# Four of the seven sums of an FFN block's products are formed in PSUM, and ScalarE copies them out

## The chip, the core and the metric

The kernel runs as one program on one core of a Trainium2 chip. The metric is the device time of that program in microseconds (us); less is better. The engines are named as in the profile: PE is TensorE, DVE is VectorE, ACT is ScalarE, POOL is GpSimd, SP issues the DMAs. SBUF is the working memory, PSUM the accumulators that PE writes.

## The reference, cut to what matters

The reference is one layer of a network: three token mixers (SSD, mLSTM, GLA), a gated merge, an output projection, then a SwiGLU FFN on 512 latent tokens with 1024 channels, and a last norm. Only the first half of the FFN is touched:

```
h = rmsnorm(x) modulated            # 512 tokens x 1024 channels
g, u = split(h @ W_in)              # 2816 columns each
a = silu(g) * u                     # then a @ W_out, the residual, the last norm
```

The kernel takes the 2816 columns as 22 blocks of 128 (blocks f = 0 to 21): a block has 128 columns of the gate g and 128 of the other factor u, over all 512 tokens.

## The kernel before, in words

Every number that PE multiplies is split into a high part (a cast by ACT to the type that PE multiplies fast) and a low part (what the cast left out, a subtraction on DVE or POOL). A product of two split operands takes three matmuls: high by high, high by low, low by high.

Blocks 0 and 1 are plain products (`halves()`). Blocks 2 to 21 (`for f in range(FC, KF)`, lines L1852 and after) save multiplications. With the block's weights as four quadrants A11, A12, A21, A22 (g or u columns by lower or upper channels), POOL forms the sums S1 = A21 + A22, S2 = S1 - A11, S3 = A11 - A21 and S4 = A12 - S2 (`weight_sums`, line L1635, 128x512 each; `FE1 = "GGGG"` puts all four on POOL). Of the eight matrices, seven are multiplied with a matching sum of tokens: A11, S1, S2, A12, S3, A22, S4. A product is 12 matmuls of 128x256 (`product`, L1849), so PE issues 84 matmuls in an iteration. The four results of a block (g and u, each for the lower and the upper 256 tokens, `lo` and `hi`) are sums of these seven products:

```
m  = A11;  r = m + S2;  v = r + S3
g[lo] = m + A12          g[hi] = r + S1 + S4
u[lo] = v + A22          u[hi] = v + S1
```

Ahead of each product `prepare()` issues one weight sum of the next block and `part(p)` for the product four places on (`FD = 4`): ACT casts the high part (L1806 in the kernel before, L1810 in the one after), and DVE or POOL subtracts for the low part (L1807, then L1811) as the letter of `FE2` says (V is DVE, G is POOL; the letter stands for the place in `order`). After the last product of an iteration `gate()` forms tanh(g/2) on ACT (L1769) and two products on DVE (L1770 and L1772, 128x512). For f below `FE0 = 4` it also splits its result at once (a cast on ACT, L362, and a subtraction, L363).

Weights, their sums and their parts live in 23 tiles of 128x512 called `w0` to `w22`, taken and given back in a ring: a cast, a sum or a subtraction that writes such a tile waits for the last reader of what stood there. In PSUM there are three tiles called `acc` and five called `bank`.

PE runs in the order of the program text. The other engines' instructions are put in an order by a scheduler before the program is built. That order is fixed, and each engine takes its own instructions in it, one by one, so whatever stands behind a waiting instruction waits too.

Of the kernel before, what the change touches and what calls it, by code (L numbers as in the profile page):

```python
# [9 lines left out]
F32 = mybir.dt.float32  # L10
# [4 lines left out]
OP = mybir.AluOpType  # L15
# [25 lines left out]
KV = 6  # L41
# [16 lines left out]
FE2 = "VVGVVGV"  # L58
# [34 lines left out]
class Slots:  # L93
    """A unit's share of the working tiles of phase one; what it puts back it can take again."""
# [18 lines left out]
    def pieces(self, c):  # L113
        """A tile of class c, cut into tiles of 512 columns."""
        t = self.get(c)
        return [t[:, j:j + 512] for j in range(0, SIZE[c] - 511, 512)]
# [11 lines left out]
    def close(self, *keep):  # L128
        """Everything is given back but for the tiles kept."""
        names = {t.tensor.name for t in keep}  # L130
        for n in [n for n in self.out if n not in names]:
            c, i = self.out.pop(n)
            self.net.free[c].append(i)
        for c, z in self.own.items():
            self.net.free[c].extend(z)
            z.clear()


class Net:
# [18 lines left out]
    def crow(self, name, n):  # L158
        """A row of constants on every partition."""
# [39 lines left out]
    def block(self, key):  # L199
        """The weight block of a key, split; fetched before if it was announced."""  # L200
# [7 lines left out]
    def fetch(self, key, now=True, pieces=None):  # L208
        """Starts to load a weight block, or some pieces of it; gives the functions that split them."""
# [35 lines left out]
    def jobs(self, queue, gens=None, then=()):  # L245
        """Runs jobs (weight block, function, ...) in order, the next block on its way, and
        carries the scans on between them."""
# [36 lines left out]
    def ready(self):  # L284
        """The next job: of those that can run, the first whose weights are here."""
# [7 lines left out]
    def push(self, jobs):  # L293
        """Jobs to be run next, behind those of the block that is on its way."""
# [17 lines left out]
    def dense(self, *parts, ks=None):  # L312
        """parts: (PSUM, weights, first column, last, tokens (high, low), first, last)."""
# [23 lines left out]
    def load_x(self):  # L337
        """The residual stream, where the context was."""
# [8 lines left out]
    def tok(self, W, i):  # L347
        """Tokens of tile i (context 0, 1, latents 2..5) on partitions, 256 columns."""
# [23 lines left out]
    def rstd_gen(self, sq, n, scale, cb, rb):  # L372
        """1 / rms of n tokens, on every partition (in rb), from tiles of squares."""
# [25 lines left out]
    def silu_c(self, c):  # L399
        """c (1 + tanh(c / 2)) of the two modulation vectors, on every partition; rows of 128, an  # L400
        identity behind them."""
# [18 lines left out]
    def modulate(self, k, s, silu):  # L420
        """Shift and scale of channels 128 k .. of one vector, by VectorE."""
# [14 lines left out]
    def modulate_pe(self, sc, ws):  # L436
        """Shift and scale of the channels from 128 KV of both vectors, by TensorE."""
# [20 lines left out]
    def scale_in(self, x, n, s, k, H, L, rb, eng):  # L458
        """The modulated norm of channels 128 k .., split."""
# [13 lines left out]
    def conv(self, acc, p, n, w, cc):  # L473
        """SAME convolution of 5 taps over the free axis, scaled by 1/2."""
# [16 lines left out]
    def gates(self):  # L491
        """Columns: decays of the SSD heads, forward and backward (32), of the mLSTM heads (8); the
        latter's input gates behind them. Tokens on partitions, tiles 0, 1 context, 2..5 latents."""
# [154 lines left out]
    def turn_rows(self, own, R, E, n, name):  # L648
        """Two sets of columns as rows over the latents, in DRAM."""
# [379 lines left out]
    def head_turn(self, own, ht, w, columns):  # L1029
        """Channels of a head on partitions, times the norm's gain; from column to row order."""  # L1030
# [257 lines left out]
    def prepare(self, b, Y, H, L, own):  # L1288
        """Splits the output of branch b, channels as they come."""
# [100 lines left out]
    def rstd2(self, c):  # L1390
        """1 / rms of 256 tokens from c on, from the sums of squares."""
# [4 lines left out]
    def late(self):  # L1396
        """The rest of the modulation of the latents."""
# [18 lines left out]
    def startup(self):  # L1416
        """The modulated inputs, and block after block of their channels the first products."""
# [144 lines left out]
    def add_square(self, m, x, c0, c1):  # L1562
        """Adds block m of the channels to the sum of squares, the last one kept apart."""
# [8 lines left out]
    def scale2(self, c, sv, h):  # L1572
        """The modulated norm before the FFN of 256 tokens from c on, in h and split."""
# [15 lines left out]
    def token_sums(self, h):  # L1589
        """With B11, B12 / B21, B22 the quadrants (channels, tokens) of h: T1 = B12 - B11,  # L1590
        T2 = B22 - T1, T3 = B22 - B12 and T4 = B21 - T2, split; per pair of channel blocks
        the tiles (T1, T3) and (T4, T2)."""
# [17 lines left out]
    def weight_sums(self, f, out):  # L1610
        """The quadrants (columns, channels) A11, A12 / A21, A22 of an FFN block and
        S1 = A21 + A22, S2 = S1 - A11, S3 = A11 - A21, S4 = A12 - S2, in steps."""
# [27 lines left out]
    def aup(self, up):  # L1640
        """The decays' weights of a head, three times: their low parts once and the high ones twice."""
# [5 lines left out]
    def small(self, p, c0, c1):  # L1647
        """The rows of the decays, three times: their high parts twice and the low ones."""
# [307 lines left out]
def lay_out(i):  # L1956
# [5 lines left out]
    A = {}  # L1962
# [67 lines left out]
```

## Time and profile before

| what | us |
|---|---|
| three runs | 1529.51, 1531.4, 1534.36 |
| median of them | 1531.4 |
| span of the profiled execution, first to last instruction | 1529.1 |
| FFN-in for blocks 2 to 21 in it, first to last copy at L1858 | 1165.06 to 1387.95 |
| one iteration in its steady part (L1858 at 1270.46, then at 1282.15) | 11.69 |
| DVE, PE, POOL, ACT busy in 1200 to 1250 of it | 49.83, 44.10, 42.35, 20.72 |

The profile gives one execution, by its span; the time of an execution that the runs report is of the same size (the span is 0.4 below the fastest run and 2.3 below the median), so differences worked out inside the span are added to the median. The granted TensorE clock was 0.973 on the mean of the span and 1.00 in the stretch from 1200 to 1250.

### The profile page before, as it was taken

The numbers are of one execution on the slowest core, as the hardware profiler recorded it, in microseconds if no ns is written. First come the engines' busy times: TensorE is split into PE (matmuls) and PEld (weight loads), VectorE is DVE, ScalarE is ACT, GpSimd is POOL, SyncE is SP. The second block draws the span as 40 slices with busy tenths as digits, with TensorE's granted clock in tenths as the row PEclk, the third lists the DMA queues.
The fourth block names the chain that finished last, engine by engine and source line by source line (L and its number), as shares of the span: only waits on it lengthen the run. The fifth ranks groups of instructions, "written<-read, shape, count | busy, mean of one in ns | idle before, by whom it ended". The sixth has DMA issues, their size and how long they took to land.

```text
span 1529.1 us, 22249 instructions
## 1 busy us (share of the span) xinstructions
PE 1406.8 (92%) x8044; PEld 1204.6 (79%) x8044; DVE 1033.0 (68%) x1783; ACT 644.0 (42%) x1191; POOL 587.2 (38%) x465
## 2 busy tenths in 40 slices
PE   5898999999999999998997789899998888888997
PEld 3687889887788886887796767677798888887887
DVE  7958463869684658786666765435369999999332
ACT  4464464553244443334454443333355343436231
POOL 4423432324222123221226353134457888881011
PEclk9998999999999999999999999999989999999999
DMA  6532323233443234354455566666322233223331
GB/s 258 189 105 84 106 69 97 72 97 97 137 126 103 78 96 129 88 129 127 159 173 171 175 210 211 197 201 215 117 77 83 83 94 100 84 84 113 90 90 66
DMA packets 99022, 190.39 MB, mean 125 GB/s; under 512 B 10752, under 2 KB 19472, under 8 KB 97760
## 3 DMA queue, kind: packets, MB, share of 16 engines
q1 hardware_dynamic: 98912, 188.97, 39.8%
q8 instruction: 63, 1.03, 0.3%
q14 instruction: 47, 0.39, 0.1%
HBM read 167.27 MB, written 21.14 MB: 123 GB/s over the span
## 4 chain that ended last, share of the span: by engine, by line
PE 53%; DVE 19%; DMA 8%; issue 6%; ACT 5%; POOL 4%; SPq 0%; DVEq 0%; ACTq 0%; POOLq 0%
PE acc L318 28%; PE acc L1884 7%; PE acc L357 7%; DVE w L1807 6%; DMA w<-in_w_main_dram 4%; PE bank L318 2%; DVE ft L1770 2%; DMA w<-in_w_b_dram 1%; ACT w L1806 1%; ACT w L215 1%; DVE w L217 1%; DMA t<-in_wmodT_dram 1%; PE bank L974 1%; POOL row L1160 1%; DMA gd<-xk 1%
## 5 line engine op out<-in xcount | busy, mean ns | idle before, releaser
L217 POOL TENSOR_TENSOR w<-w,w 128x512 fp32r<-128x512 f32 x125 | 176.2, 1409 | 572.8 <-ACT w L215 499.4
L318 PE MATMUL acc<-hlh,w 128*128 128x512 f32 (+1 forms) x1160 | 390.7, 406 | 5.5 <-ACT hlh L465 1.9
L215 ACT CAST w<-w 128x512 fp32r<-128x512 f32 (+1 forms) x302 | 183.2, 613 | 382.9 <-DMA w<-in_w_main_dram 182.6
L217 DVE TENSOR_TENSOR w<-w,w 128x512 fp32r<-128x512 f32 x177 | 138.6, 785 | 202.7 <-ACT w L215 168.6
L318 PEld LDWEIGHTS acc<-hlh,w 128*128 128x128 f32 x1160 | 225.3, 194 | 59.9 <-ACT hlh L465 2.2
L318 PE MATMUL acc<-hll,w 128*128 128x512 f32 (+1 forms) x576 | 230.7, 400 | 3.7 <-DVE hll L471 1.5
L1635 POOL TENSOR_TENSOR w<-w,w 128x512 f32<-128x512 f32 x80 | 135.7, 1717 | 2.7 <-DMA w<-in_w_ffs_dram 1.9
L318 PEld LDWEIGHTS acc<-hll,w 128*128 128x128 f32 x576 | 111.8, 194 | 28.7 <-DVE hll L471 1.9
L1807 DVE TENSOR_TENSOR w<-w,w 128x512 fp32r<-128x512 f32 x100 | 124.0, 1241 | 0.0
L318 PE MATMUL acc<-t,w 128*128 128x512 f32 x440 | 111.2, 401 | 7.4 <-DVE t L363 2.7
L318 PEld LDWEIGHTS acc<-t,w 128*128 128x128 f32 x440 | 83.2, 190 | 28.9 <-DVE t L363 4.3
L1806 ACT CAST w<-w 128x512 fp32r<-128x512 f32 x140 | 79.1, 618 | 60.9 <-DVE w L1807 50.2
L357 PE MATMUL acc<-w,hlh 128*128 128x256 f32 x512 | 96.6, 289 | 0.0
L1849 PE MATMUL bank<-th,w 128*128 128x256 f32 x480 | 93.4, 283 | 0.1
L1849 PE MATMUL acc<-hlh,w 128*128 128x256 f32 x280 | 59.6, 290 | 29.9 <-DVE w L1807 29.9
L357 PEld LDWEIGHTS acc<-w,hlh 128*128 128x128 f32 x512 | 81.6, 194 | 3.0 <-ACT t L920 1.6
L480 DVE SCALAR_TENSOR_TENSOR cacc<-acc,c_scanc,cacc 128x510 f32<-128x510 f32 (+3 forms) x124 | 77.7, 631 | 6.7 <-ACT cacc L476 5.8
L1849 PEld LDWEIGHTS bank<-th,w 128*128 128x128 f32 x480 | 77.3, 190 | 0.5 <-DVE w L1807 0.3
L1807 POOL TENSOR_TENSOR w<-w,w 128x512 fp32r<-128x512 f32 x40 | 61.5, 1538 | 38.1 <-ACT w L1806 36.2
L357 PE MATMUL acc<-w,hll 128*128 128x256 f32 x256 | 73.4, 287 | 0.0
L1849 PEld LDWEIGHTS acc<-hlh,w 128*128 128x128 f32 x280 | 46.0, 190 | 33.7 <-DVE w L1807 33.7
L1849 PE MATMUL bank<-tl,w 128*128 128x256 f32 x240 | 67.8, 282 | 0.0
(453 smaller groups left out, 3089.5 us busy)
## 6 DMA issues: line engine op xcount, KB each, us to landing
w<-in_w_main_dram SPq DMA_DIRECT2D x180, 256.0 KB, 3.4
w<-in_w_ffs_dram SPq DMA_DIRECT2D x80, 256.0 KB, 3.1
t<-in_wmodT_dram SPq DMA_DIRECT2D x32, 512.0 KB, 4.0
w<-in_w_b_dram SPq DMA_DIRECT2D x48, 256.0 KB, 3.5
xk<-gd SPq DMA_DIRECT2D x40, 256.0 KB, 3.5
w<-in_w_ffo_dram SPq DMA_DIRECT2D x40, 256.0 KB, 2.6
row<-rows SPq DMA_DIRECT2D x16, 512.0 KB, 5.5
wmod<-in_wmod_dram SPq DMA_DIRECT2D x6, 1024.0 KB, 8.3
```

Source lines behind the costliest of these rows:

```text
L215: self.S.copy(h, w)
L217: self.LE[self.wcount % len(self.LE)].tensor_sub(l, w, h.bitcast(F32))
L318: self.T.matmul(dst, w[:, m0:m1], x[:, c0:c1], start=(k == 0 and j == 0), stop=(k == nk - 1 and j == 2))
L357: self.T.matmul(p, x[:, t0:t0 + 128], w, start=(k == 0 and j == 0), stop=(k == KT - 1 and j == 2))
L480: V.scalar_tensor_tensor(acc[:, o0:o1], p[:, o0 + d:o1 + d], w[:, cc, j:j + 1], acc[:, o0:o1], op0=OP.mult, op1=OP.add)
L974: T.matmul(bs[:, :257], kw[d], v[:, 2 + i], start=True, stop=True)
L1635: getattr(next(eng), op)(new(z), x, y)
L1770: V.scalar_tensor_tensor(t, t, 1.0, g, op0=OP.add, op1=OP.mult)
L1806: S.copy(H, x)
L1807: le[p % 7].tensor_sub(L, x, H.bitcast(F32))
L1849: T.matmul(dst, x, y, start=(k == 0 and j == 0), stop=(k == 3 and j == 2))
L1884: T.matmul(po, w, x[:, c0:c1], start=(f == 0 and j == 0), stop=(f == KF - 1 and j == 2))
```

## The change

- The seven products come in another order: A11, S1, S2, A12, S3, S4, A22 instead of A11, S2, S1, A12, S3, A22, S4.
- Three tiles of PSUM are used in an iteration instead of seven. In X the products A11, S2, S3 and A22 are added up one after the other by PE (the first matmul of a later product doesn't clear the tile), so that X holds m, then r, then v, then u[lo]. In Y, S1 and then S4 are added up. Z holds A12.
- ACT copies X out three times (m, r, v) and Y once (`p5`, the product S1) between the products; before, it copied m alone. PE may not add the next product to X or Y until the copy has read it.
- DVE keeps two additions that read PSUM (g[lo] = m + Z, g[hi] = r + Y) where it had seven, and gets one whose operands both lie in SBUF (v + p5, 128x256, which is u[hi]).
- The second instruction of the gate is cut into two of 256 columns: the first reads u[lo] in X (in PSUM), the second reads u[hi] in SBUF. Before, it was one of 512 columns with both operands in SBUF.
- `FE2` is `"VVVGVVG"` instead of `"VVGVVGV"`: read against the two orders, POOL subtracted for S1 and A22 before, and does for A12 and A22 now; DVE does for the other five.
- The tile `fu` is gone, and comments are.

```diff
-FE2 = "VVGVVGV"
+FE2 = "VVVGVVG"
...
-                def gate(f, g, u):
+                def gate(f, g, *u):
...
-                    V.scalar_tensor_tensor(act[f], t, 0.5, u, op0=OP.mult, op1=OP.mult)
+                    c = 0
+                    for z in u:
+                        cs = slice(c, c + z.shape[-1])
+                        V.scalar_tensor_tensor(act[f][:, cs], t[:, cs], 0.5, z, op0=OP.mult, op1=OP.mult)
+                        c = cs.stop
...
-                order = ("A11", "S2", "S1", "A12", "S3", "A22", "S4")
+                order = ("A11", "S1", "S2", "A12", "S3", "S4", "A22")
...
-                def product(f, n, dst):
-                    dst = dst[:, :256]
+                def product(f, n, dst, first=True):
...
-                            T.matmul(dst, x, y, start=(k == 0 and j == 0), stop=(k == 3 and j == 2))
+                            T.matmul(dst, x, y, start=(first and k == 0 and j == 0), stop=(k == 3 and j == 2),
+                                     skip_group_check=True)
...
-                    S.copy(m, product(f, "A11", self.acc_bank()))
-                    V.tensor_add(r, m, product(f, "S2", self.bank()))
-                    p5 = product(f, "S1", self.bank())
-                    V.tensor_add(g[:, lo], m, product(f, "A12", self.acc_bank()))
-                    V.tensor_add(g[:, hi], r, p5)
-                    V.tensor_add(v, r, product(f, "S3", self.bank()))
-                    V.tensor_add(u[:, hi], v, p5)
-                    V.tensor_add(u[:, lo], v, product(f, "A22", self.acc_bank()))
-                    V.tensor_add(g[:, hi], g[:, hi], product(f, "S4", self.bank()))
-                    gate(f, g, u)
+                    X, Y, Z = (z[:, :256] for z in (self.acc_bank(), self.bank(), self.bank()))
+                    product(f, "A11", X)
+                    S.copy(m, X)
+                    product(f, "S1", Y)
+                    S.copy(p5, Y)
+                    product(f, "S2", X, False)
+                    S.copy(r, X)
+                    product(f, "A12", Z)
+                    V.tensor_add(g[:, lo], m, Z)
+                    product(f, "S3", X, False)
+                    S.copy(v, X)
+                    product(f, "S4", Y, False)
+                    V.tensor_add(g[:, hi], r, Y)
+                    V.tensor_add(v, v, p5)
+                    product(f, "A22", X, False)
+                    gate(f, g, X, v)
```

ACT's order in one iteration of the kernel before, block 11, from the tanh of block 10 on (each row: line, operation, tile written, tiles read, size; a number behind a name tells one use of a tile from another):

```order
L1769 ACTIVATE ft_11686<-fg_11538 128x512
L1858 COPY fm_11693<-acc_11696 128x256
L1806 CAST w3_11768<-w7_11655 128x512
L1806 CAST w4_11789<-w12_11747 128x512
L1806 CAST w7_11834<-w19_11661 128x512
L1806 CAST w0_11816<-w5_11727 128x512
L1806 CAST w10_11862<-w13_11766 128x512
L1806 CAST w15_11882<-w22_11659 128x512
L1806 CAST w18_11902<-w6_11787 128x512
```

ACT's order in the same iteration of the changed kernel:

```order
L1769 ACTIVATE ft_11649<-fg_11506 128x512
L1810 CAST w5_11713<-w14_11474 128x512
L1864 COPY fm_11656<-acc_11660 128x256
L1810 CAST w3_11732<-w18_11619 128x512
L1866 COPY fp_11659<-bank_11661 128x256
L1810 CAST w8_11751<-w0_11692 128x512
L1810 CAST w18_11794<-w15_11625 128x512
L1868 COPY fr_11657<-acc_11660 128x256
L1810 CAST w2_11776<-w12_11711 128x512
L1872 COPY fv_11658<-acc_11660 128x256
L1810 CAST w20_11824<-w13_11730 128x512
L1810 CAST w10_11843<-w4_11749 128x512
```

Three copies were put between the casts; the cast of A22 now stands directly behind the tanh, and the copy of r behind the fourth cast, which writes the tile `w18` (before, the third cast, which writes `w7`, had only casts behind it).

DVE's order in the same iteration of the kernel before, from the second product of the gate on:

```order
L1772 SCALAR_TENSOR_TENSOR a10_11689<-ft_11686,fu_11539 128x512
L1807 TENSOR_TENSOR w17_11769<-w7_11655,w3_11768 128x512
L1859 TENSOR_TENSOR fr_11694<-fm_11693,bank_11714 128x256
L1807 TENSOR_TENSOR w8_11790<-w12_11747,w4_11789 128x512
L1862 TENSOR_TENSOR fg_11691<-fr_11694,bank_11734 128x256
L1861 TENSOR_TENSOR fg_11691<-fm_11693,acc_11753 128x256
L1807 TENSOR_TENSOR w21_11835<-w19_11661,w7_11834 128x512
L1863 TENSOR_TENSOR fv_11695<-fr_11694,bank_11774 128x256
L1807 TENSOR_TENSOR w12_11863<-w13_11766,w10_11862 128x512
L1864 TENSOR_TENSOR fu_11692<-fv_11695,bank_11734 128x256
L1865 TENSOR_TENSOR fu_11692<-fv_11695,acc_11795 128x256
L1866 TENSOR_TENSOR fg_11691<-fg_11691,bank_11821 128x256
```

DVE's order in the same iteration of the changed kernel, from the first product of the gate on:

```order
L1770 SCALAR_TENSOR_TENSOR ft_11649<-ft_11649,fg_11506 128x512
L1775 SCALAR_TENSOR_TENSOR a10_11652<-ft_11649,acc_11511 128x256
L1775 SCALAR_TENSOR_TENSOR a10_11652<-ft_11649,fv_11509 128x256
L1811 TENSOR_TENSOR w17_11733<-w18_11619,w3_11732 128x512
L1811 TENSOR_TENSOR w6_11752<-w0_11692,w8_11751 128x512
L1870 TENSOR_TENSOR fg_11655<-fm_11656,bank_11662 128x256
L1811 TENSOR_TENSOR w11_11777<-w12_11711,w2_11776 128x512
L1875 TENSOR_TENSOR fv_11658<-fv_11658,fp_11659 128x256
L1811 TENSOR_TENSOR w0_11825<-w13_11730,w20_11824 128x512
L1874 TENSOR_TENSOR fg_11655<-fr_11657,bank_11661 128x256
L1811 TENSOR_TENSOR w12_11844<-w4_11749,w10_11843 128x512
```

Seven short additions with a PSUM operand (`bank`, `acc`) became two, and one addition between two SBUF tiles (`fv`, `fp`) stands between the third and the fourth subtraction; the first subtraction behind the gate reads `w18`, the tile that ACT's fourth cast writes next.

POOL's order in the same iteration of the changed kernel: two sums (S1, S2), the subtraction for A22, two sums (S3, S4), the subtraction for the next block's A12.

```order
L1635 TENSOR_TENSOR w0_11692<-w11_11621,w22_11623 128x512
L1635 TENSOR_TENSOR w12_11711<-w0_11692,w18_11619 128x512
L1811 TENSOR_TENSOR w1_11714<-w14_11474,w5_11713 128x512
L1635 TENSOR_TENSOR w13_11730<-w18_11619,w11_11621 128x512
L1635 TENSOR_TENSOR w4_11749<-w15_11625,w12_11711 128x512
L1811 TENSOR_TENSOR w7_11795<-w15_11625,w18_11794 128x512
```

Before, POOL's row was subtraction, sum, subtraction, three sums. The subtraction for A12 writes the tile `w7`, which PE reads in product S3 of the same iteration (as `w7_11675`).

## Rows read from the trace of the kernel before

**Rows 1.** The page's first line.

```profile
span 1529.1 us, 22249 instructions
```

**Rows 2.** Busy time by windows: us, PE, PEld, DVE, ACT, POOL, PE clock, DMA.

```profile
1200.00:1250.00 50.00, 44.10 (x366) 43.28 (x366) 49.83 (x59) 20.72 (x40) 42.35 (x26) 1.00 0.31 95
```

**Rows 3.** Groups by shape, 1140 to 1390: busy us, mean ns, idle before.

```profile
L1635 POOL TENSOR_TENSOR w<-w,w 128x512 f32<-128x512 f32 x77 | 131.2, 1725 | 2.0 <-DMA w<-in_w_ffs_dram 1.9
L1807 DVE TENSOR_TENSOR w<-w,w 128x512 fp32r<-128x512 f32 x100 | 124.0, 1241 | 0.0
```

**Rows 4.** Waits, 1160 to 1370: total us, times, longest.

```profile
PE acc L1849 <- DVE w L1807: 24.3, 17, 1.7
```

**Rows 5.** Timeline of DVE: start, length, line, operation.

```profile
1262.23 1.75 DVE L1807 TENSOR_TENSOR w<-w,w 128x512 fp32r<-128x512 f32 x1
...
1264.24 0.68 DVE L1807 TENSOR_TENSOR w<-w,w 128x512 fp32r<-128x512 f32 x1
1264.84 0.41 DVE L1862 TENSOR_TENSOR fg<-fr,bank 128x256 f32<-128x256 f32 x1
1265.17 0.41 DVE L1861 TENSOR_TENSOR fg<-fm,acc 128x256 f32<-128x256 f32 x1
1265.51 1.69 DVE L1807 TENSOR_TENSOR w<-w,w 128x512 fp32r<-128x512 f32 x1
...
1267.45 1.44 DVE L1807 TENSOR_TENSOR w<-w,w 128x512 fp32r<-128x512 f32 x1
...
1269.81 0.78 DVE L1807 TENSOR_TENSOR w<-w,w 128x512 fp32r<-128x512 f32 x1
1270.59 1.71 DVE L1770 SCALAR_TENSOR_TENSOR ft<-ft,fg 128x512 f32<-128x512 f32 x1
1272.33 1.66 DVE L1772 SCALAR_TENSOR_TENSOR a<-ft,fu 128x512 f32<-128x512 f32 x1
1273.91 1.75 DVE L1807 TENSOR_TENSOR w<-w,w 128x512 fp32r<-128x512 f32 x1
```

**Rows 6.** Timeline of POOL, with the idle time before in brackets.

```profile
1265.35 1.30 POOL L1807 TENSOR_TENSOR w<-w,w 128x512 fp32r<-128x512 f32 x1 [1.91 <-ACT w L1806]
1266.61 1.73 POOL L1635 TENSOR_TENSOR w<-w,w 128x512 f32<-128x512 f32 x1
1268.30 1.74 POOL L1807 TENSOR_TENSOR w<-w,w 128x512 fp32r<-128x512 f32 x1
1270.01 5.11 POOL L1635 TENSOR_TENSOR w<-w,w 128x512 f32<-128x512 f32 x3
1277.03 1.29 POOL L1807 TENSOR_TENSOR w<-w,w 128x512 fp32r<-128x512 f32 x1 [1.91 <-ACT w L1806]
```

**Rows 7.** Timeline of ACT in the steady part.

```profile
1264.06 2.70 ACT L1806 CAST w<-w 128x512 fp32r<-128x512 f32 x5 [3.35 <-DVE w L1807]
...
1270.46 0.35 ACT L1858 COPY fm<-acc 128x256 f32<-128x256 f32 x1
...
1282.15 0.36 ACT L1858 COPY fm<-acc 128x256 f32<-128x256 f32 x1
```

**Rows 8.** Timeline of ACT at the stage's start.

```profile
1177.53 0.35 ACT L1858 COPY fm<-acc 128x256 f32<-128x256 f32 x1
...
1181.10 0.62 ACT L362 CAST ah<-ft 128x512 fp32r<-128x512 f32 x1 [2.70 <-DVE ft L1772]
```

**Rows 9.** Timeline of DVE and POOL at 131 and at 839.

```profile
131.50 0.40 DVE L544 TENSOR_TENSOR t<-t,t 128x240 f32<-128x240 f32 x1
131.78 1.70 POOL L217 TENSOR_TENSOR w<-w,w 128x512 fp32r<-128x512 f32 x1 [3.75 <-ACT w L215]
131.82 0.40 DVE L545 TENSOR_TENSOR t<-t,t 128x240 f32<-128x240 f32 x1
...
838.65 0.68 DVE L217 TENSOR_TENSOR w<-w,w 128x512 fp32r<-128x512 f32 x1
...
839.15 1.32 POOL L217 TENSOR_TENSOR w<-w,w 128x512 fp32r<-128x512 f32 x1 [2.56 <-issue]
839.25 2.85 DVE L1085 TENSOR_TENSOR_SCAN t<-mask,t 128x774 f32<-128x774 bf16 x1
```

More of the change, by code (lines that the diff above doesn't have):

```diff
@@ L1848, in product @@
                         for j, (x, y) in enumerate(((w, h), (w, l), (v, h))):
-                            T.matmul(dst, x, y, start=(k == 0 and j == 0), stop=(k == 3 and j == 2))
+                            T.matmul(dst, x, y, start=(first and k == 0 and j == 0), stop=(k == 3 and j == 2),
+                                     skip_group_check=True)
                     self.wput(*slots)
                     next(prep, None)
-                    return dst
                 for f in range(FC, KF):
                     lo, hi = slice(0, 256), slice(256, 512)
-                    g, u = (sp.tile([128, 512], F32, name=n, bufs=2) for n in ("fg", "fu"))
-                    m, r, v = (sp.tile([128, 256], F32, name=n, bufs=2) for n in ("fm", "fr", "fv"))
-                    S.copy(m, product(f, "A11", self.acc_bank()))
-                    V.tensor_add(r, m, product(f, "S2", self.bank()))
-                    p5 = product(f, "S1", self.bank())
-                    V.tensor_add(g[:, lo], m, product(f, "A12", self.acc_bank()))
-                    V.tensor_add(g[:, hi], r, p5)
-                    V.tensor_add(v, r, product(f, "S3", self.bank()))
-                    V.tensor_add(u[:, hi], v, p5)
-                    V.tensor_add(u[:, lo], v, product(f, "A22", self.acc_bank()))
-                    V.tensor_add(g[:, hi], g[:, hi], product(f, "S4", self.bank()))
-                    gate(f, g, u)
+                    g = sp.tile([128, 512], F32, name="fg", bufs=2)
+                    m, r, v, p5 = (sp.tile([128, 256], F32, name=n, bufs=2) for n in ("fm", "fr", "fv", "fp"))
+                    X, Y, Z = (z[:, :256] for z in (self.acc_bank(), self.bank(), self.bank()))
[14 more added lines that the diff above has]
+                    gate(f, g, X, v)
                 for f in range(FE0, KF):
@@ L1920, in final @@
         for h in range(4):
-            o = self.sp.tile([128, 2, 256], F32, name=("ft", "fu")[h % 2], bufs=2)
+            o = self.sp.tile([128, 2, 256], F32, name=("ft", "fg")[h % 2], bufs=2)
             for j in range(2):
```

## The prediction

> **What bounds the kernel now.** I read the page first for the span [rows 1]; the change touches only FFN-in, some 220 us of it. Then the windows: in that stage DVE is busy 49.83 of 50 us, PE 44.10 and POOL 42.35, at a full clock [rows 2]. Read alone, this says that DVE is the bound and that additions taken off it are time won. The groups speak against that: DVE's subtraction of 128x512 takes 1241 ns on the mean [rows 3], while one of the same shape takes 0.68 where it ran alone (at 1264.24) [rows 5]. So I went to the two timelines. From POOL's subtraction at 1265.35 on, DVE and POOL take turns: POOL's 1.30 ends at 1266.65, DVE's subtraction that began at 1265.51 ends at 1267.20, 0.55 later; POOL's next (from 1266.61) ends at 1268.34, 1.14 later; DVE's (from 1267.45) ends at 1268.89, 0.55 later, and so on [rows 5, 6]. An operation of DVE with both operands in SBUF and one of POOL never progress together; each turn is about 1.15 for POOL and 0.55 for DVE. Much of DVE's "busy" is waiting for its turn. The additions that read PSUM don't take part: 0.41, and 0.33 start to start (the one at 1264.84 is followed by another at 1265.17) [rows 5].
>
> One iteration is thus a chain of turns. From POOL's start at 1265.35 to the end of DVE's subtraction at 1273.91 + 1.75 = 1275.66 it has POOL's first 1.30, five more turns of POOL and six of DVE: 1.30 + 5 x 1.15 + 6 x 0.55 = 10.35, and the rows give 10.31. Then it leaves the pair: ACT's cast waited 3.35 for just this subtraction, which frees its tile (seen an iteration earlier: DVE ends at 1262.23 + 1.75 = 1263.98, ACT starts at 1264.06), and two casts later POOL can start its next subtraction at 1277.03, having idled 1.91 [rows 5 to 7]. This detour is 1277.03 - 1275.66 = 1.37. Together 11.68; the copies of m are 1282.15 - 1270.46 = 11.69 apart [rows 7]. PE is no bound, it waits for DVE's subtractions, 24.3 us in 17 waits [rows 4]; a product is 12 x 44.10 / 366 = 1.45, seven are 10.1.
>
> **The change part by part.**
>
> *Five additions with a PSUM operand leave DVE, 5 x 0.33 = 1.65 per iteration, 33 us in 20.* They ran beside POOL's turns: between 1264.84 and 1270 POOL works on while DVE does them [rows 5, 6]. I take them at nothing. If that cover were absent the gain would be the 33.
>
> *The addition v + p5, both in SBUF,* joins the turns with 256 columns. No row has it; its bounds are nothing (the engine waits anyhow) and a full turn, 0.55. I take half, 0.28. *The gate's second product:* of 0.55 in the turns, the half that reads PSUM leaves and the other stays, 0.28. So DVE's turns are 6 x 0.55 + 2 x 0.28 = 3.86 against 7 x 0.55 = 3.85 before, POOL's stay 6 x 1.15 = 6.9. The sum, 10.75, is what the pair needs in either kernel, 0.94 below the 11.69. What the change can win is in the gaps, 0.94 x 17 = 16 us at most.
>
> *The order of the turns.* By the order of the changed kernel, from POOL's subtraction for A12: 1.30, v + p5 0.28, sum S1 1.15, subtraction 0.55, sum S2 1.15, subtraction 0.55. Here the gate's first product stands right behind that subtraction on DVE, and if it goes on at once it takes 0.60 (the pitch from 1264.24 to 1264.84); then POOL's A22 subtraction 1.15, the SBUF half of the gate 0.28, sum S3 1.15, DVE's subtraction that reads `w18` 0.55. Sum 1.30 + 0.28 + 1.15 + 0.55 + 1.15 + 0.55 + 0.60 + 1.15 + 0.28 + 1.15 + 0.55 = 8.71. The last turns (sum S4 and a subtraction) fall into the detour.
>
> *The detour grows.* That subtraction frees the tile for ACT's fourth cast, as its counterpart did before. But now the copy of r stands behind this cast, PE may not add product S3 to X before it, and POOL's subtraction for A12 writes the tile that product S3 reads last. The chain: 0.08 to ACT, cast 0.54 (2.70 / 5), copy 0.35 [rows 7], a hand-over to PE, product 1.45, a hand-over to POOL. The hand-overs I take at 0.13 each, what is left of the old detour after 0.08 and two casts (1.37 - 0.08 - 1.16). Sum 0.08 + 0.54 + 0.35 + 0.13 + 1.45 + 0.13 = 2.68. An iteration is then 8.71 + 2.68 = 11.39, 0.30 less than 11.69. Over the 17 steady intervals: -5.1 us.
>
> The Trainium skill, "Perfetto Trace Analysis", section Matmuls, says that independent matmul groups should rotate through different PSUM banks, so that a copy out of one overlaps the matmuls of the next. The old code does so and the new one chains four products in X. Counted by the rule with nothing overlapped, three copies of 0.35 and two hand-overs of 0.13 each, 0.61 x 3 x 20, would cost 37 us; the order of products here puts another product (1.45) between two of X, which covers 0.61, unless ACT is late.
>
> *The start.* While f < 4 the gate ends in a split whose cast (L362) waits for the gate on DVE, 2.70 [rows 8]. Before, the copy of m stood ahead of it (1177.53 against 1181.10). Two such gates lie in the loop, of blocks 2 and 3. In the changed order the next block's copy of m stands behind this cast, and PE's S2 waits for it. I take 2.5 each, +5; bounds 0 (PE had lost that time anyhow) and 2.7 each, plus one wait of 3.35 in the first iteration, where fewer turns are queued, 8.8.
>
> *The rest:* PSUM has tiles to spare with three in use instead of seven, no DMA is added, the matmuls are the same 84. The three added copies cost ACT 0.35 each [rows 7], at 20.72 of 50 busy [rows 2]: nothing, but for the detour counted above.
>
> The sum: -5.1 + 5 = about 0, on the span of 1529.1 and so on the median of 1531.4. **Forecast: no change, 1531.4 us.** Own range of this case 1526 to 1536: the steady gain could be 0.1 more or less per interval (1.7), the start -5 to +3.8.
>
> **The rivals.**
>
> *POOL takes the pair first (slower).* The place: DVE's subtraction that ends the turn before the gate's first product. The addition g[hi] stands ahead of this subtraction, and ACT's tanh and the A22 cast follow it, 0.41, the tanh at the pitch of a cast of its size, 0.54, the cast 0.62 [rows 8] and two hand-overs that I estimate at 0.05 each, 1.67 from its start; the subtraction, waiting for POOL, starts 0.33 after it and lasts 1.44, 1.77. So POOL's A22 subtraction asks for the pair some 0.1 before DVE is through, and the gate's product asks as DVE goes on. If POOL goes first, its 1.15 comes ahead of the gate, and the chain to the subtraction that frees `w18` becomes 1.30 + 0.28 + 1.15 + 0.55 + 1.15 + 0.55 + 1.15 + 0.55 + 1.15 + 0.28 + 1.15 + 0.55 = 9.81; with 2.68, 12.49, +0.80 per iteration. 17 x 0.80 + 5 = +18.6: 1550. What decides is who wins when POOL asks about 0.1 early. In the one near case POOL began 0.12 before DVE's operation ended (131.78 against 131.90), DVE's next went on at 0.40 and POOL took 1.70, so DVE won; where POOL began 0.18 before the end (839.15 against 839.33), it took 1.32 and DVE's next 2.85, so POOL won [rows 9]. 0.1 lies on DVE's side, by little. Chance 0.28.
>
> A rule beside it: the Trainium skill, "SBUF — State Buffer", section Who interferes with whom, has the shared port pair as an exclusive lock, taken by DVE operations with two SBUF inputs, and lets issue order decide who blocks; the turns of rows 5 and 6 agree (1.15 and 0.55). Taken by the word, POOL's request, issued earlier, would win; the row at 131.78 does not agree with that reading, the one at 839.15 does.
>
> *DVE is the bound after all (faster).* If the chain closes up without the longer detour, the 16 us of gaps are won: 1531.4 - 16 = 1515, or 1520 with the start's +5. For it: DVE's 49.83 of 50, and the 1.65 that leave. Against it: the turns, and that ACT's cast still waits for one subtraction. Chance 0.10.
>
> *PE waits for ScalarE in each chain (slower).* In an iteration the copies of m and v have one product of cover as well; were one of them late as the copy of r is, by another 2.68 - 1.37 = 1.31, that is 1.31 x 17 = 22 us, 1553. For it: ACT is served in order and waits 3.35 at a time [rows 7]. Against it: only one cast per iteration waits so long. Chance 0.05.
>
> *Nothing but noise around the forecast:* 0.57.
>
> **How the numbers follow.** A measurement of this kernel tells changes from 0.3%, 4.6 us, on. The forecast's case (0.57) lies within it but for its edges, 0.06 to the faster side and 0.03 to the slower. So faster 0.10 + 0.06 = 0.16, same 0.48, slower 0.28 + 0.05 + 0.03 = 0.36. The range leaves out the faster rival (0.10) and the upper tail of the slower ones: 1525 to 1551.
>
> **What would show it.** Right: in 1200 to 1350 copies of m 11.3 to 11.5 apart; DVE's additions with PSUM gone and its busy time lower by no more than the stretched operations take; ACT's fourth cast waiting some 2 us with the copy of r behind it and PE waiting about 1.5 for that copy; first two intervals longer than before. Rival one: intervals of 12.5, POOL's A22 subtraction at 1.3 and the gate's first product at 1.7 or more. Rival two: intervals below 11. Wrong altogether: stretched additions that read PSUM, or a clock below 1.00 in the stage.

## The result and the profile after

The changed kernel takes 1554.46 us on the median of four runs (1551.62 to 1558.02), the kernel before 1532.88 in the same comparison: the ratio is 1.0167, with a 95% interval of 1.014 to 1.0194. It is slower by about 22 us. I had forecast no change, 1531.4, and a range to 1551; the time lies on the far side of the range, at the price of the first rival (1550). The ratios in this document leave out runs that took over 1.5% longer than the fastest of the same kernel, which concerns two of the ten runs with S2 and S4 on POOL.

The span, to compare with [rows 1]:

```profile
span 1549.9 us, 22177 instructions
```

It grew by 20.8, the clock's mean over it is 0.968 (0.973 before). Busy time in two windows of the same stage as [rows 2], with the same columns:

```profile
1200.00:1250.00 50.00, 42.61 (x340) 41.78 (x338) 43.62 (x45) 22.96 (x47) 35.40 (x24) 0.97 0.31 94
1250.00:1300.00 50.00, 43.64 (x336) 42.82 (x336) 41.97 (x44) 22.96 (x49) 35.46 (x24) 0.93 0.24 76
```

DVE is busy 43.62 in place of 49.83, and POOL 35.40 in place of 42.35: both now stand idle at times. More than half of this is only that an iteration is longer. For one iteration, with the lengths below, DVE's busy time is 43.62 x 12.55 / 50 = 10.95 against 49.83 x 11.69 / 50 = 11.65, which is 0.70 less. No engine is near 50: what bounds the stage is a chain of waits through all of them. The longest waits in 1160 to 1400, total, times, longest (left out: PE's weight loads, which wait together with its products):

```profile
POOL w L1811 <- PE acc L1853: 59.3, 18, 5.9
ACT w L1810 <- POOL w L1635: 46.1, 16, 3.8
...
PE acc L1853 <- ACT fr L1868: 29.3, 16, 2.4
```

The first and the last are new: POOL waits for PE's product, PE for ScalarE's copy of r. They are the detour of the prediction. Its beginning, on DVE, ScalarE and PE:

```profile
1272.76 1.75 DVE L1811 TENSOR_TENSOR w<-w,w 128x512 fp32r<-128x512 f32 x1
1274.59 0.62 ACT L1810 CAST w<-w 128x512 fp32r<-128x512 f32 x1 [3.30 <-POOL w L1635]
1275.53 0.39 PE L1853 MATMUL acc<-th,w 128*128 128x256 f32 x1 [2.34 <-ACT fr L1868]
```

The view puts the cast's wait down to POOL's sums, but these ended at 1273.97. DVE's subtraction, which reads the tile that the cast writes, ended at 1274.51, 0.08 before the cast begins, the same distance as in [rows 5, 7]. So I read it as the wait for DVE. ScalarE's copies of m give the length of an iteration, as in [rows 7]:

```profile
1269.38 0.36 ACT L1864 COPY fm<-acc 128x256 f32<-128x256 f32 x1
...
1281.95 0.36 ACT L1864 COPY fm<-acc 128x256 f32<-128x256 f32 x1
...
1295.45 0.38 ACT L1864 COPY fm<-acc 128x256 f32<-128x256 f32 x1 [0.79 <-PE acc L1853]
...
1307.11 0.37 ACT L1864 COPY fm<-acc 128x256 f32<-128x256 f32 x1
```

They are 12.57, 13.50 and 11.66 apart. Fourteen steady intervals, 1206.54 to 1382.25, take 12.55 on the mean, against 11.69 before (1200.27 to 1363.99): 14 x 0.86 = 12.0 us. The first three take 44.0 (17.78, 15.17, 11.05) against 35.2: 8.8. The last two take 25.6 against 24.0: 1.6. That is 22.4, less the 2.5 by which the first copy comes earlier.

The place of the first rival, on DVE and on POOL (start, length):

```profile
1280.80 1.45 DVE L1811 TENSOR_TENSOR w<-w,w 128x512 fp32r<-128x512 f32 x1
1282.17 1.79 DVE L1770 SCALAR_TENSOR_TENSOR ft<-ft,fg 128x512 f32<-128x512 f32 x1
1284.07 0.42 DVE L1775 SCALAR_TENSOR_TENSOR a<-ft,acc 128x256 f32<-128x256 f32 x1
1284.40 0.99 DVE L1775 SCALAR_TENSOR_TENSOR a<-ft,fv 128x256 f32<-128x256 f32 x1
```

```profile
1277.27 1.29 POOL L1811 TENSOR_TENSOR w<-w,w 128x512 fp32r<-128x512 f32 x1 [3.30 <-PE acc L1853]
1278.62 3.08 POOL L1635 TENSOR_TENSOR w<-w,w 128x512 f32<-128x512 f32 x2
1282.13 1.29 POOL L1811 TENSOR_TENSOR w<-w,w 128x512 fp32r<-128x512 f32 x1 [0.43 <-ACT w L1810]
1283.37 3.16 POOL L1635 TENSOR_TENSOR w<-w,w 128x512 f32<-128x512 f32 x2
```

POOL's subtraction for A22 begins at 1282.13, 0.12 before DVE's subtraction ends (1280.80 + 1.45 = 1282.25), and runs at its own 1.29. The gate's first product begins at 1282.17 and takes 1.79 where it could take 0.68: it stood behind POOL. It is so at 13 of the 18 gates from 1176 to 1395, with a lead of 0.12 to 0.14. At the other five POOL's second sum comes late, and the gate's product takes 1.77 or 1.78 behind that sum, ahead of the A22 subtraction (last section). The gate's half that reads PSUM takes 0.42 beside POOL's sums, the half that reads SBUF 0.99.

### The profile page after: what moved, and what is told of

Same layout as the page of the kernel before. It is cut to its first block, busy times and chain, and to the rows that moved or that the text cites. A ratio compares the mean times of both kernels' runs of the same rounds, so it can differ in the third digit from the quotient of the medians.

```text
span 1549.9 us, 22177 instructions
## 1 busy us (share of the span) xinstructions
PE 1414.6 (91%) x8044; PEld 1213.1 (78%) x8044; DVE 1015.0 (65%) x1723; ACT 665.4 (43%) x1251; POOL 570.2 (37%) x465
## 4 chain that ended last, share of the span: by engine, by line
PE 58%; DVE 11%; DMA 9%; POOL 7%; ACT 5%; issue 5%; SPq 0%; DVEq 0%; POOLq 0%; ACTq 0%
PE acc L318 28%; PE acc L1894 8%; PE acc L1853 6%; DMA w<-in_w_main_dram 5%; PE acc L357 4%; PE bank L1853 3%; POOL w L1635 3%; DMA t<-in_wmodT_dram 2%; PE bank L318 2%; DVE w L217 1%; ACT w L215 1%; POOL row L1160 1%; DVE w L1811 1%; DVE xk L1411 1%; ACT w L1810 1%
## 5 line engine op out<-in xcount | busy, mean ns | idle before, releaser
L217 POOL TENSOR_TENSOR w<-w,w 128x512 fp32r<-128x512 f32 x125 | 175.6, 1405 | 572.9 <-ACT w L215 496.3
L318 PEld LDWEIGHTS acc<-hlh,w 128*128 128x128 f32 x1160 | 225.6, 195 | 60.0 <-ACT hlh L465 2.2
L217 DVE TENSOR_TENSOR w<-w,w 128x512 fp32r<-128x512 f32 x177 | 138.1, 783 | 203.3 <-ACT w L215 154.7
L1853 PE MATMUL acc<-th,w 128*128 128x256 f32 x480 | 105.6, 302 | 41.6 <-ACT fr L1868 30.4
L1635 POOL TENSOR_TENSOR w<-w,w 128x512 f32<-128x512 f32 x80 | 123.9, 1559 | 9.9 <-DMA w<-in_w_ffs_dram 4.6
L1811 DVE TENSOR_TENSOR w<-w,w 128x512 fp32r<-128x512 f32 x100 | 119.9, 1212 | 9.6 <-issue 7.2
L1853 PEld LDWEIGHTS acc<-th,w 128*128 128x128 f32 x480 | 84.5, 204 | 45.9 <-ACT fr L1868 33.9
L1810 ACT CAST w<-w 128x512 fp32r<-128x512 f32 x140 | 86.6, 620 | 64.6 <-POOL w L1635 46.1
L1811 POOL TENSOR_TENSOR w<-w,w 128x512 fp32r<-128x512 f32 x40 | 54.8, 1370 | 69.6 <-PE acc L1853 59.3
L1853 PE MATMUL acc<-tl,w 128*128 128x256 f32 x240 | 71.2, 297 | 0.0
L1411 DVE SCALAR_TENSOR_TENSOR xk<-t 128x1024 bf16<-128x1024 f32 x32 | 44.1, 1378 | 31.5 <-DMA t<-in_wmodT_dram 31.5
L318 PE MATMUL acc<-row,w 128*128 128x512 f32 (+1 forms) x312 | 63.9, 361 | 0.6 <-DVE row L366 0.5
```

The source lines that it names most:

```text
L217: self.LE[self.wcount % len(self.LE)].tensor_sub(l, w, h.bitcast(F32))
L318: self.T.matmul(dst, w[:, m0:m1], x[:, c0:c1], start=(k == 0 and j == 0), stop=(k == nk - 1 and j == 2))
L1411: V.scalar_tensor_tensor(junk, w, 0.5, sc, op0=OP.mult, op1=OP.mult, accum_out=self.mod[:, 0, j:j + 1])
L1635: getattr(next(eng), op)(new(z), x, y)
L1810: S.copy(H, x)
L1811: le[p % 7].tensor_sub(L, x, H.bitcast(F32))
```

## The experiments

The question: is it the one lost turn, POOL's A22 subtraction ahead of the gate's first product (theory A), PE's chain in X with the copies in it (theory B), or the order of products and the letters (theory C)?

**POOL asks later.** An operation is added to POOL, none is taken away:

```diff
+                tick = sp.tile([128, 1], F32, name="tick")
...
+                    if p % 7 == 6:
+                        G.tensor_copy(tick, H.bitcast(F32)[:, :1])
                     le[p % 7].tensor_sub(L, x, H.bitcast(F32))
```

> The changed kernel with one copy of 128x1 by POOL, which reads the A22 cast, ahead of POOL's subtraction for A22: POOL's long operation asks for the pair some 0.1 us later, and POOL has more to do. Theory A (turns: the 12.56 us of an iteration come from POOL's A22 subtraction taking the pair just ahead of the gate's first product): DVE's product now goes first, the iteration falls by 0.8 to 1.1 us to 11.4 to 11.8, the time by 14 to 19 us to 1535 to 1541. Theory B (chain: PE may not add the next product to X before ScalarE's copy, whoever has the turn): nothing changes or it gets slower by the 20 added operations, 1554 to 1558.

Measured: 1532.72, ratio to the kernel before 1.0013 (0.9997 to 1.0028). Twenty added operations win back the whole loss of 22 us. Its DVE and POOL at the same place:

```profile
1281.65 1.45 DVE L1814 TENSOR_TENSOR w<-w,w 128x512 fp32r<-128x512 f32 x1
1283.03 0.68 DVE L1770 SCALAR_TENSOR_TENSOR ft<-ft,fg 128x512 f32<-128x512 f32 x1
```

```profile
1282.97 0.19 POOL L1813 COPY tick<-w 128x1 f32<-128x1 f32 x1 [0.41 <-ACT w L1811]
1283.11 1.77 POOL L1814 TENSOR_TENSOR w<-w,w 128x512 fp32r<-128x512 f32 x1
```

The small copy stands where the A22 subtraction stood, 0.13 before DVE's subtraction ends (1283.10), and is over in 0.19. The gate's product goes at 0.68, POOL's long operation begins 0.14 later than its place and waits in its turn. It is so at all 17 gates that such a copy stands ahead of. The iterations are 11.44 to 11.51 long. This is the kernel of my forecast: 11.39 worked out, 1531.4 forecast.

**The control.** The same copy ahead of the subtraction for A12:

```diff
-                    if p % 7 == 6:
+                    if p % 7 == 3:
                         G.tensor_copy(tick, H.bitcast(F32)[:, :1])
```

> A control: the changed kernel with the same 128x1 copy by POOL, which reads the cast, but ahead of the subtraction for A12 instead of the one for A22. Theory A (the turn ahead of the gate): nothing there depends on 0.1 us, POOL's A22 subtraction still takes the pair, an iteration of 12.4 to 12.7, 1551 to 1557. Rival (any small operation of POOL that breaks the rhythm helps): 1532 to 1540.

Measured: 1552.2, ratio 1.0148 (1.0112 to 1.0183). The interval overlaps that of the changed kernel (1.014 to 1.0194): the same added work in another place gives back nothing that can be told from noise, and the iterations are 12.49 on the mean. It is the place, ahead of the gate, that counts. As the whole cause, theory B falls with these two: the chain in X is the same in both.

**The order and the letters, without the chain.**

```diff
-FE2 = "VVGVVGV"
+FE2 = "VVVGVVG"
...
-                order = ("A11", "S2", "S1", "A12", "S3", "A22", "S4")
+                order = ("A11", "S1", "S2", "A12", "S3", "S4", "A22")
...
-                    V.tensor_add(r, m, product(f, "S2", self.bank()))
                     p5 = product(f, "S1", self.bank())
+                    V.tensor_add(r, m, product(f, "S2", self.bank()))
```

with A22 and S4 exchanged likewise, all additions on DVE.

> The kernel before with the new order of products and the new letters, all additions still on DVE, no product added up in PSUM, one copy by ScalarE. Theory B (chain in PSUM) puts the whole loss in the chain: 1530 to 1535. Theory C (the order of products and the letters alone bring the loss): 1550 and more. Theory A (turns): the copy of r no longer stands between the fourth cast and product S3, so the detour of 2.75 us falls; if DVE then gets its turn ahead of A22 it is faster than before, 1518 to 1528, if not about as before, 1528 to 1538.

Measured: 1531.59, ratio 0.9996 (0.9977 to 1.0014). Theory C falls: order and letters alone lose nothing. The steady iterations are shorter than before, 11.19 on the mean in place of 11.69, but the first ones are longer (13.86 and 12.82 against 12.47 and 11.00). DVE does not get its turn here either:

```profile
1271.10 1.45 DVE L1807 TENSOR_TENSOR w<-w,w 128x512 fp32r<-128x512 f32 x1
1272.47 1.80 DVE L1770 SCALAR_TENSOR_TENSOR ft<-ft,fg 128x512 f32<-128x512 f32 x1
```

```profile
1272.43 1.30 POOL L1807 TENSOR_TENSOR w<-w,w 128x512 fp32r<-128x512 f32 x1 [0.43 <-ACT w L1806]
```

POOL's A22 subtraction leads by 0.12 again (1271.10 + 1.45 = 1272.55) and goes first, at 17 of 18 gates. So it is the second branch of theory A that is met (1528 to 1538), and the band of theory B as well. This sharpens the answer: the 22 us need the lost turn and the chain with its detour together. With the turn won back by the late request, or with the chain undone here, they are gone. What the turn alone is worth without the chain no run shows, since none wins it there.

**A22 on DVE.** In the changed kernel:

```diff
-FE2 = "VVVGVVG"
+FE2 = "VVVGVVV"
```

> The changed kernel with the subtraction for A22 on DVE instead of POOL (letters VVVGVVV). Theory A: there is no A22 request of POOL to win the turn, POOL has one turn of 1.15 less, DVE one of 0.55 more, but the sum S3 now asks for the same turn: an iteration of 11.7 to 12.2, 1537 to 1549. Theory B: PE's wait for the copy of r stays, 1552 to 1558.

Measured: 1548.46, ratio 1.0113 (1.0086 to 1.014), at the upper end of A's band. Taking the request away gives little, where delaying it gave all. The gate's product loses its turn all the same: at 16 of 18 gates it takes 1.75 to 1.79 behind a sum of POOL, at the other two 0.68. DVE has one turn more, and POOL's wait for product S3 is longer than in the changed kernel, 76.9 us in 18 waits against 59.3. The iterations run between 11.31 and 13.60, 12.38 on the mean, above A's 12.2.

**A12 on DVE.** This takes away the end of the detour, POOL's wait for the tile that product S3 reads:

```diff
-FE2 = "VVVGVVG"
+FE2 = "VVVVVVG"
```

> The changed kernel with the subtraction for A12 on DVE and the one for A22 left on POOL (letters VVVVVVG). POOL then no longer waits for PE's product S3, which frees the tile of A12. Theory A with the detour as I summed it (2.7 us per iteration through cast, copy, product S3 and POOL): the detour is gone, an iteration of 10.6 to 11.1, 1517 to 1527, although A22 is still asked for at the same place. Theory B (the chain in X, and PE's wait for the copy of r in it): PE still waits for the copy of r, 1548 to 1556. If the turn at A22 alone matters and not the detour: 1550 to 1556.

Measured: 1524.24, ratio 0.9951 (0.9929 to 0.9974). The steady iterations are 10.87 to 10.96. PE at product S3, and POOL:

```profile
1277.00 0.38 PE L1853 MATMUL acc<-th,w 128*128 128x256 f32 x1 [0.68 <-ACT fr L1868]
```

```profile
1272.26 1.74 POOL L1811 TENSOR_TENSOR w<-w,w 128x512 fp32r<-128x512 f32 x1
1273.95 3.16 POOL L1635 TENSOR_TENSOR w<-w,w 128x512 f32<-128x512 f32 x2
1280.06 3.13 POOL L1635 TENSOR_TENSOR w<-w,w 128x512 f32<-128x512 f32 x2 [2.95 <-PE bank L1853]
```

PE's wait for the copy of r is down to 0.68. The A22 subtraction now asks while POOL's sums are still on (1272.26, with no idle time before it), so it no longer stands at the place where both engines ask. The expectation had it there still, so its number came true in part by another path. The gate's product still takes 1.77 (at 1281.96), behind POOL's second sum, and the iteration is short all the same. With the chain in place the changed kernel can be faster than before: the chain by itself is not the loss.

**The old letters in the new order.** In the changed kernel, S2 and S4 on POOL:

```diff
-FE2 = "VVVGVVG"
+FE2 = "VVGVVGV"
```

> The changed kernel with the letters of the kernel before, VVGVVGV, which in the new order put S2 and S4 on POOL: A12 and A22 go to DVE, POOL keeps two subtractions. Theory A (turns): no A22 request of POOL stands ahead of the gate, and POOL's subtractions no longer wait for product S3's tile, as where A12 alone was moved (an iteration of 10.90 there): 10.8 to 11.2 us per iteration, 1518 to 1530. Theory B (chain in X, the added copies): the wait for the copy of r stays in each iteration, 1545 to 1556.

Measured: 1533.68, but the ten runs lie between 1520.01 and 1548.54; ratio 1.0013 (0.9974 to 1.0052). The steady iterations of the profiled execution, whose span is 1527.7, are 10.93 to 11.01, as A has it; one at the start took 15.22, the last 14.50. The median of all ten misses A's band; without the two longest runs, 1546.06 and 1548.54, it is 1529.12, at the band's upper end. The spread says that executions differ in what they fall into. Inconclusive; the next experiment shows what that can be.

**S4 alone on POOL.** In the changed kernel:

```diff
-FE2 = "VVVGVVG"
+FE2 = "VVVVVGV"
```

> The changed kernel with POOL subtracting for S4 alone (letters VVVVVGV). Theory A: POOL has five turns as where A22 alone was left on POOL (1524), and none of them waits for PE's product S3 or stands ahead of the gate: 10.7 to 11.1 us per iteration, 1516 to 1526. If what counts is only how much POOL is relieved, the same as with A22 on POOL, 1522 to 1527.

Measured: 1524.25 (1516.87 to 1536.29), ratio 0.9953 (0.9921 to 0.9986), the same as with A22 alone on POOL, so both readings fit. The profiled execution, of span 1528.6, has, after its first two, iterations of 13.08, 13.52, 13.52 and 11.88 and then, up to the last, 10.90 to 11.13. Windows of 10 us of it (the columns of [rows 2]):

```profile
1200.00:1210.00 10.00, 8.25 (x65) 8.04 (x64) 8.46 (x9) 3.97 (x10) 6.15 (x5) 0.94 0.36 104
1210.00:1220.00 10.00, 9.47 (x72) 9.27 (x70) 8.10 (x9) 4.35 (x9) 7.37 (x5) 0.89 0.03 11
1220.00:1230.00 10.00, 8.77 (x61) 8.77 (x62) 6.80 (x11) 4.97 (x10) 4.33 (x4) 0.83 0.30 99
1230.00:1240.00 10.00, 8.35 (x71) 8.15 (x70) 8.18 (x12) 4.97 (x10) 5.37 (x4) 1.00 0.37 105
1240.00:1250.00 10.00, 9.29 (x78) 9.09 (x78) 9.26 (x12) 5.25 (x11) 7.04 (x5) 1.00 0.35 107
```

The two iterations of 13.52, from 1201.70 to 1228.74, lie where the clock is 0.83 to 0.94; that of 11.88, to 1240.62, lies mostly at 1.00, as do the short ones behind it. That PE's slow products keep the waits long, and these the clock low, until a turn falls otherwise, is argued from these rows and not tested.

**The copy of r by DVE.** In the changed kernel:

```diff
-                    S.copy(r, X)
+                    V.tensor_copy(r, X)
```

> The changed kernel with the copy of r (product S3 waits for it) by DVE instead of ScalarE. Theory A: the copy gets rid of the blocked cast, but lands behind DVE's own turns; the A22 turn is lost as before: 12.2 to 12.6 us per iteration, 1548 to 1556. Rival (ScalarE's queue is the cause: the copy of r behind a cast that waits 3.3 us): PE no longer waits 2.3 us for it, an iteration of 11.2 or less, 1525 to 1535.

Measured: 1562.7 (1551.32 to 1567.61), ratio 1.0205 (1.0141 to 1.0269). Without the blocked cast ahead of the copy the iterations are 12.75 on the mean (1203.15 to 1381.70, 14 of them), and PE waits for the copy on DVE instead, 27.5 us in 15 waits. So this change did not take the wait away, and alone it does not clear ScalarE's queue. The late request does: it leaves that queue as it is and wins the time back. That the lost turn makes r late on either engine is argued. The median is above A's band by 7; the profiled execution, at 1549.5, is not.

**The start.** The kernel with A12 on DVE, and the splits of blocks 2 and 3 put off until after the loop:

```diff
-FE0 = 4
+FE0 = 2
```

> The kernel with the subtraction for A12 on DVE (1524.24), and the gates of blocks 2 and 3 not split at once but after the loop, as all later ones are (FE0 = 2). This takes the two casts that wait for the gate out of the loop, ahead of the next block's copy of m. If they are the start's cost, the first two intervals fall from 17.1 and 12.6 to about 13 and 11, some 5 us; two splits more are then to be done after the loop, at 1.2 to 1.4 us each where they are not hidden: 1518 to 1523. If the start's cost lies elsewhere (fewer queued turns, the tiles of the first weights): 1524 to 1528.

Measured: 1518.36, ratio 0.9928 (0.9901 to 0.9956), 5.9 less than without. The intervals of the two ratios overlap; the place shows in the trace, where the first two intervals are 12.97 and 10.92, in place of 17.14 and 12.59: 5.8. The term of the start is where the sum put it. This kernel is faster than both the kernel before and the changed one.

**The chain's worth in it.** That kernel with all additions on DVE again and no chain, as in the experiment on the order and the letters:

```diff
-                    product(f, "S2", X, False)
-                    S.copy(r, X)
+                    V.tensor_add(r, m, product(f, "S2", self.bank()))
...
-                    product(f, "S3", X, False)
-                    S.copy(v, X)
+                    V.tensor_add(v, r, product(f, "S3", self.bank()))
```

> The fastest kernel (1518.36: A12 subtracted by DVE, late splits of blocks 2 and 3) with the chains undone: all additions on DVE, no product added up in PSUM, one copy by ScalarE. If the chains win nothing by themselves, since the additions that they take off DVE ran beside POOL's turns: 1516 to 1523. If the chains are what lets the moved subtraction win, by freeing DVE for it: DVE has 1.65 us more per iteration and seven subtractions of 0.6 in its turns, 11.4 to 11.8 per iteration, 1529 to 1538.

Measured: 1548.97, ratio 1.0143 (1.0093 to 1.0193), iterations of 12.4. Against the kernel with the chain, 31 us are lost. That the chain wins nothing by itself falls. The loss is larger than the band, 1.5 an iteration against 0.5 to 0.9. POOL, with five operations an iteration, idles between them for a DMA of weights and for ScalarE's cast:

```profile
1276.74 3.46 POOL L1635 TENSOR_TENSOR w<-w,w 128x512 f32<-128x512 f32 x2 [1.63 <-DMA w<-in_w_ffs_dram]
1282.67 1.46 POOL L1807 TENSOR_TENSOR w<-w,w 128x512 fp32r<-128x512 f32 x1 [2.47 <-ACT w L1806]
```

So with these letters and the late splits the chain is worth 31 us, and with the letters VVVGVVG and the early ones it costs 23 (1554.46 against 1531.59). The parts of this change have no price of their own; which of the 31 belongs to which wait stays open.

## Why the prediction was wrong

- *What bounds the kernel.* Right: turns of DVE and POOL. DVE's busy time fell by 6.21 us in 50, by 0.70 in an iteration, and the kernel got slower.
- *The order of the turns.* Here is the step that failed: "if it goes on at once it takes 0.60", for the gate's first product. It did not go on at once: it took 1.79. I had the place and the 0.1 us lead (measured 0.12), and "0.1 lies on DVE's side, by little" gave the turn to DVE by the one near row at 131.78, where POOL's lead was 0.12 as well. In the changed kernel POOL wins with that lead. The rows at 839 had it right. Two more places in the trace of before, which I had not read, say the same: at 439.13 and 687.04 POOL led by 0.20 and 0.16, and DVE's next took 1.35 and 1.31, where the one just before it had taken 0.34 and 0.28. The late request shows the step as the cause: delayed by 0.14, the iteration is 11.48 (forecast 11.39), the time 1532.72 (forecast 1531.4). The Trainium skill, "SBUF — State Buffer", section Who interferes with whom, read by the word (issue order decides who blocks), had this place right, and I set a single row of 240-column operations against it; this case's traces agree with it in FFN-in (POOL's subtraction starts at 1282.13, the gate's product at 1282.17), and not everywhere (last section).
- *What the lost turn costs depends on the chain.* The sum had 1.10 between the two orders (9.81 less 8.71), and 12.55 less 11.48 is 1.07. But this is its price with the detour behind it. Without the chain the same turn is lost, and an iteration takes 11.19, less than before.
- *The price of losing the turn.* 12.49 worked out, 12.57 measured where the clock stayed up, 12.55 on the mean. The chain, with the rows above: POOL 1.29 to 1278.56, v + p5 0.28, S1 1.16, and so on to DVE's subtraction that frees `w18`.
- *The detour.* 2.68 in the sum; from that subtraction's end (1274.51) to POOL's start (1277.27) it is 2.76. Moving A12 off POOL gives 10.9, inside the 10.6 to 11.1 worked out from it, but the place of the A22 request changed as well, so that run gives no price of the detour alone.
- *The five additions at nothing.* Right here: without the change of turns (the late request) the steady gain is 0.21 of the 0.30 forecast, and not the 1.65 taken off DVE. Not a rule: without the chain, the fastest kernel loses 31.
- *The start.* +5 in the sum; +4.8 with the late request (40.0 against 35.2 for three intervals), +8.8 in the changed kernel, where the lost turn comes on top. In both the first copy comes 2.5 earlier than before, which the sum did not have and which takes back half of the 5. In the changed kernel the cast of the split stands ahead of the copy of m, as the sum had it:

```profile
1179.80 0.62 ACT L362 CAST ah<-ft 128x512 fp32r<-128x512 f32 x1 [3.34 <-DVE ft L1775]
1180.32 0.36 ACT L1864 COPY fm<-acc 128x256 f32<-128x256 f32 x1
```

  Putting the splits off was tried in the kernel with A12 on DVE alone, where it took 5.8 off the first two intervals.
- *PE waits for ScalarE in each chain.* This rival meant the copies of m and v, and does not hold: PE waits for m four times (11.2 us in all), and the list has no wait for v. The wait for r was in the sum. It is 1.8 a time (29.3 in 16 waits) and in part a consequence of the lost turn: the late request keeps the copies in place, and the wait falls to 1.2 (22.4 in 19).
- *The rule on rotating PSUM banks* (the Trainium skill, "Perfetto Trace Analysis", section Matmuls), as the prediction counted it with nothing overlapped, would have made the chain cost 37 us by itself. The runs show no such fixed cost: 23 us are lost by the chain with one set of letters, 31 won with another.
- *What would show it.* All signs of the first rival are there: intervals of 12.55, POOL's A22 subtraction at 1.29, the gate's first product at 1.79. A clock below 1.00 in the stage was named as a sign that all is wrong: it is 0.93 to 0.97 in the windows, but over pairs of intervals it costs nothing (last section).
- *The range* ended at 1551 on a slow case worked out at 1550. That case was right in its mechanism, and its 18.6 us stand against 19.9 inside the trace (22.4 less 2.5); the measurement's own scatter alone (1551.62 to 1558.02) needed more room.

## What to carry to other kernels

Where two engines take turns at something, an iteration is a chain of turns, and work taken off one of them is won only where it shortens that chain: write the turns down in order before costing anything. Then look for places where both ask within 0.1 or 0.2 us of each other; such a place can be worth a turn per iteration, 1.07 us here, so forecast it as two outcomes of like weight, not as one with a tail. What it comes to hangs on what stands behind it: without the chain the same lost turn left the kernel no slower than before. So take away each suspect alone before calling one the cause. A version whose time hangs on such a place is better rearranged (another engine for one operation, splits put off) than tuned around: here that took the kernel from 1554 to 1518.

## What the runs showed of the hardware that was not expected

- 0.14 us decided 22 us: with the same lead of 0.12 us DVE kept the pair at 131.78 [rows 9] and lost it in FFN-in. What differs there is 240 columns against 512, and that the DVE operation ahead had itself waited. Neither alone decides it. With S4 alone on POOL, POOL led by 0.11 behind a DVE operation of 512 columns that had not waited (1132.78, 0.68), and won; with the late splits it led by 0.14 behind another such (354.01, 0.68), and lost:

```profile
1133.35 1.28 POOL L1635 TENSOR_TENSOR w<-w,w 128x512 f32<-128x512 f32 x1 [1.04 <-DMA w<-in_w_ffs_dram]
1133.38 1.79 DVE L217 TENSOR_TENSOR w<-w,w 128x512 fp32r<-128x512 f32 x1
```

```profile
354.55 1.90 POOL L217 TENSOR_TENSOR w<-w,w 128x512 fp32r<-128x512 f32 x1 [4.29 <-ACT w L215]
354.62 0.69 DVE L765 TENSOR_TENSOR xk<-t,TC 128x512 f32<-128x512 f32 x1
```

  What does decide it stays open.
- PE's wait for r, 2.3 us long, is followed by a lower clock in some iterations and not in others. Windows of the changed kernel around the wait that ends at 1288.10:

```profile
1274.00:1276.00 2.00, 0.47 (x4) 0.47 (x4) 1.44 (x3) 1.41 (x3) 0.00 (x0) 1.00 0.58 216
1286.00:1288.00 2.00, 0.00 (x0) 0.00 (x0) 2.00 (x3) 0.85 (x3) 0.53 (x1) 0.93 0.91 288
1288.00:1291.00 3.00, 2.90 (x13) 2.91 (x14) 0.70 (x2) 0.56 (x2) 0.04 (x1) 0.50 0.19 71
```

The product after it ran at 0.50, the lower of the two levels (1.2 of 2.4 GHz), and POOL's subtraction for A12, which waits for that product, came 2.86 after PE's start (1290.96) in place of 1.74 (1277.27). After the wait that ended at 1275.53 the clock stayed at 1.00. The time came back at once: POOL's sums are late with it, the gate's product goes ahead of the A22 subtraction, which now takes the longer time,

```profile
1294.77 1.77 DVE L1770 SCALAR_TENSOR_TENSOR ft<-ft,fg 128x512 f32<-128x512 f32 x1
1295.95 1.76 POOL L1811 TENSOR_TENSOR w<-w,w 128x512 fp32r<-128x512 f32 x1
```

  the next interval is 11.66, and 13.50 + 11.66 is 25.16, two intervals of 12.58.
- The addition v + p5, 256 columns from SBUF, which no row of before showed, on DVE with A12 moved to DVE (POOL idle):

```profile
1279.21 0.42 DVE L1875 TENSOR_TENSOR fv<-fv,fp 128x256 f32<-128x256 f32 x1
```

and in the changed kernel, beside POOL's subtraction of 1277.27:

```profile
1277.68 1.16 DVE L1875 TENSOR_TENSOR fv<-fv,fp 128x256 f32<-128x256 f32 x1 [0.90 <-ACT fv L1872]
```

It takes 0.42 alone; in its turn it ends at 1278.84, 0.28 after POOL (1278.56), which is the half turn that the sum took for it.
